# Products of two groups at once in the gates stage of a two-block layer: blind prediction and result

## The chip, the cores and the metric

The kernel runs on one core of a Trainium2 chip. The metric is the device time of one execution in microseconds; a time that is compared is the median of several runs. The core has five engines that take their instructions from queues of their own, each in the order in which the program issued them: TensorE (PE in the profile, with its weight loads as PEld), VectorE (DVE), ScalarE (ACT), GpSimd (POOL) and SyncE (SP), which here only starts DMAs.

## The reference

Two transformer blocks on 256 tokens of width 1024 in float32. The first has a SwiGLU layer, a hybrid of stick-breaking attention and a state-space mixer, cross attention and a second SwiGLU layer. The second has a mixer and then an expert layer with 16384 experts of rank one, which is the part that matters here:

```python
q = (xt @ wq).reshape(t, PEER_HEADS, 2, HALF_Q)
scores = jnp.einsum('thpd,hpnd->thpn', q, keys)
s_top, i_top = lax.top_k(scores, PEER_TOPK)          # 16 of 128 keys, twice
...                                                  # 16 of the 256 sums: c_score, c_idx
expert = i1 * N_KEYS + i2                            # 8 heads x 16 experts a token
gates = jax.nn.softmax(c_score, axis=-1)
u = jnp.take(u_tab, eb, axis=0)
a = jax.nn.gelu(jnp.einsum('td,thkd->thk', xb, u), approximate=False)
w = gb * a
y = jnp.einsum('thk,thkd->td', w, jnp.take(v_tab, eb, axis=0))
```

## The kernel before, in words

The kernel doesn't gather experts. It computes the Gelu of every token with all 16384 rows of the first table (the units `pu`, 128 tiles of 128 experts), multiplies by a dense matrix of gates, mostly zeros, and multiplies the result with the whole second table (the units `pv`). X holds 128 x 128 x 256 values: first index i1's tile, partition i2, then the token.

A tile of `pu` is one call of `f_tile` (L324): 24 matmuls (L332 to L334, three for each of 8 parts of the width, since a float32 weight is split in a rounded `hi` and a rest `lo`) into one of two PSUM banks `mm`. Then ScalarE applies the Gelu (L1488 into X for tokens whose gates are not there yet, L1490 in place for the others) and VectorE multiplies the latter into X (L1491). The split of a later tile's weights is made at a tile's end: `hi` on ScalarE (L169), `lo` on VectorE (L170).

The dense gates are made beside these tiles, four tokens (a group) at a time, 64 groups, by the generator `gates` (L1366). For each token of a group GpSimd compares a row of numbers with the first index (`m1`, L1375, one-hot), ScalarE scales it by the gate's upper part (`oh`, L1377), VectorE by its lower part (`ol`, L1380), and VectorE makes the one-hot of the second index (`m2`, L1378). All this is `hot`. TensorE multiplies `oh` and `ol` with `m2` (L1388, 8 matmuls of 128 columns a group, float16) into a PSUM bank `sd`, of which there are two. Then the group is spread over X: ScalarE copies the gates of tiles that have no Gelu yet (L1396), VectorE multiplies the others into X (L1398). The tiles `m1`, `m2`, `oh` and `ol` have two buffers each.

What sets the order is a planner. Each generator has a time due. `f_tile` calls `tick(1.3)` in the middle of a tile (behind 12 matmuls) and at its end, behind the Gelu and the product and ahead of the split; a tick takes 1.3 from the time due and, as long as it isn't above zero, steps the generator and adds what that yields. A step without a number adds 3.3 here, so a group comes every 3.3 us of the planner's time. One step before issues the products of group g, then `hot` of g + 1, then the spread of g.

Of the kernel before, what the change touches and what calls it, by code (L numbers as in the profile page):

```python
# [8 lines left out]
F16 = mybir.dt.float16  # L9
I32 = mybir.dt.int32  # L10
U32 = mybir.dt.uint32
AF = mybir.ActivationFunctionType
OP = mybir.AluOpType
# [103 lines left out]
class Builder:  # L117
# [363 lines left out]
    def spread(self, hn, t, dst, col):  # L481
        self.transposes(hn[t].ap, t, dst, col)
        hn[t].free()
# [882 lines left out]
    def gates(self, kT, X):  # L1366

        nc = self.nc

        def hot(g):  # L1370
            tile = lambda name: self.pw.tile([128, 4, 128], F16, name=name, bufs=2)
            m1, m2, oh, ol = (tile(n) for n in ("m1", "m2", "oh", "ol"))
            key = lambda w, i: kT[:, w, 4 * g + i:4 * g + i + 1]
            for i in range(4):
                nc.gpsimd.tensor_scalar(m1[:, i], self.iota, key(0, i), None, op0=OP.is_equal)  # L1375
            for i in range(4):
                nc.scalar.activation(oh[:, i], m1[:, i], AF.Copy, scale=key(2, i))  # L1377
                nc.vector.tensor_scalar(m2[:, i], self.iota, key(1, i), 1.0 / self.SCALE, op0=OP.is_equal, op1=OP.mult)  # L1378
            for i in range(4):
                nc.vector.tensor_scalar(ol[:, i], m1[:, i], key(3, i), None, op0=OP.mult)  # L1380
            return (oh, ol), m2
        o = hot(0)
        yield
        for g in range(64):
            ps = self.sd()
            for i in range(4):
                for p in range(2):
                    nc.tensor.matmul(ps[:, i * 128:i * 128 + 128], o[0][p][:, i], o[1][:, i], start=(p == 0),  # L1388
                                     stop=(p == 1))
            if g < 63:  # L1390
                o = hot(g + 1)
            E = self.u_done
            pv = ps.rearrange("p (t i) -> p t i", t=4)
            x = X[:, :, 4 * g:4 * g + 4].rearrange("p i t -> p t i")
            if E < 128:
                nc.scalar.activation(x[:, :, E:128], pv[:, :, E:128], AF.Copy)  # L1396
            if E:
                nc.vector.tensor_mul(x[:, :, 0:E], pv[:, :, 0:E], x[:, :, 0:E])  # L1398
            self.g_done = 4 * g + 4
            yield  # L1400

    def peer(self):
        nc, hT = self.nc, self.uT
# [407 lines left out]
```

## Time and profile before

| | |
|---|---|
| median of 3 runs | 1656.46 us (1656.13 to 1656.62) |
| the profiled execution | 1655.53 us, its span 1653.8 us |
| PE, PEld busy | 1632.5 us (99%), 1481.6 us (90%) |
| DVE busy | 1148.0 us (69%) |
| ACT busy | 977.9 us (59%) |
| POOL busy | 268.6 us (16%) |
| DMA | 288.77 MB, mean 175 GB/s |
| chain that ended last | PE 81%, DVE 11%, ACT 3%, issue 2%, DMA 2%, POOL 1% |

Busy shares are means over the whole span. The gates stage lies between about 1024 and 1292 us from the start; GpSimd is busy almost only there. Matmuls are pipelined and their ends are modelled, so on TensorE one reads the starts: the distance from a start to the next is what a matmul costs.

### The profile page before, as it was taken

The page shows a single profiled execution, that of the slowest core. Times are in us where ns is not written, and L with a number is a line of the kernel's source. Part 1 is how long each engine was busy: PE and PEld are TensorE (multiplying, and loading weights), DVE is VectorE, ACT ScalarE, POOL GpSimd, SP SyncE. Part 2 cuts the span into 40 slices and gives each one's busy share as a digit, 9 for nine tenths or more (in the row PEclk, how much of TensorE's full clock was granted, in tenths as well). Part 3 has the DMA queues.
Part 4 walks back from the last instruction along what each step waited for, and adds up shares of the span by engine and source line. Part 5 has one row for each costly group of instructions (what it writes and reads, how often), then busy time and mean ns, then how long its engine had stood idle before and what let it go on. Part 6 is the DMA issues. An engine that isn't in the chain of part 4 may idle for free.

```text
span 1653.8 us, 29236 instructions
## 1 busy us (share of the span) xinstructions
PE 1632.5 (99%) x11102; PEld 1481.6 (90%) x11102; DVE 1148.0 (69%) x2366; ACT 977.9 (59%) x1826; POOL 268.6 (16%) x311
## 2 busy tenths in 40 slices
PE   8999999999999999999999999999999999999998
PEld 6999899988898899979889999999999888888886
DVE  6554765877756645487657998899999755555554
ACT  6443676786555544467355565888877555444454
POOL 0000000000000000000100003988888000000000
PEclk9999999999999999999999999999999999999999
DMA  7565643364524656555244555444454555555553
GB/s 280 192 208 175 227 143 116 115 202 143 179 103 154 216 190 206 177 185 197 78 140 143 192 190 192 166 163 164 161 166 153 180 205 194 194 195 193 191 191 128
DMA packets 79325, 288.77 MB, mean 175 GB/s; under 512 B 8784, under 2 KB 8912, under 8 KB 79056
## 3 DMA queue, kind: packets, MB, share of 16 engines
q1 hardware_dynamic: 77904, 281.66, 49.8%
q10 hardware_dynamic: 1280, 5.24, 1.0%
q8 instruction: 87, 1.43, 0.3%
q14 instruction: 54, 0.44, 0.1%
HBM read 285.82 MB, written 1.05 MB: 173 GB/s over the span
## 4 chain that ended last, share of the span: by engine, by line
PE 81%; DVE 11%; ACT 3%; issue 2%; DMA 2%; POOL 1%; SPq 0%; POOLq 0%; DVEq 0%; ACTq 0%
PE mm L332 12%; PE mm L334 12%; PE mm L333 12%; PE acc L349 10%; PE acc L351 10%; PE acc L353 10%; DVE lo L170 4%; PE mm L303 2%; PE mm L300 2%; PE mm L299 2%; DMA raw<-ws 2%; PE sd L1388 1%; ACT hi L169 1%; DVE m L1378 1%; DVE X L1260 1%
## 5 line engine op out<-in xcount | busy, mean ns | idle before, releaser
L170 DVE TENSOR_TENSOR lo<-raw,hi 128x1024 fp32r<-128x1024 f32 x414 | 506.6, 1228 | 237.5 <-ACT hi L169 236.1
L332 PE MATMUL mm<-uT,hi 128*128 128x256 f32 x2104 | 597.1, 284 | 2.1 <-DVE X L1491 1.7
L334 PE MATMUL mm<-uT,lo 128*128 128x256 f32 x2104 | 587.1, 279 | 0.0
L333 PE MATMUL mm<-uT,hi 128*128 128x256 f32 x2104 | 586.9, 279 | 0.0
L169 ACT ACTIVATE hi<-raw 128x1024 fp32r<-128x1024 f32 x414 | 436.3, 1058 | 214.9 <-PE acc L353 171.1
L332 PEld LDWEIGHTS mm<-uT,hi 128*128 128x128 f32 x2104 | 397.1, 189 | 4.9 <-DVE X L1491 2.6
L333 PEld LDWEIGHTS mm<-uT,hi 128*128 128x128 f32 x2104 | 397.1, 189 | 0.8
L334 PEld LDWEIGHTS mm<-uT,lo 128*128 128x128 f32 x2104 | 397.0, 189 | 0.0
L1375 POOL TENSOR_SCALAR m<-iota,kT 128x128 f16<-128x128 f16 x256 | 233.2, 927 | 197.8 <-DVE kT L1358 149.9
L438 POOL TENSOR_TENSOR hr<-hv,mhalf 128x1 f32<-128x1 f32 x26 | 14.4, 552 | 816.3 <-DVE hv L437 816.3
L349 PE MATMUL acc<-hi,wf 128*128 128x512 f32 x384 | 118.9, 390 | 0.0
L351 PE MATMUL acc<-lo,wf 128*128 128x512 f32 x384 | 118.7, 389 | 0.0
L353 PE MATMUL acc<-hi,wf 128*128 128x512 f32 x384 | 118.5, 389 | 0.0
L170 DVE TENSOR_TENSOR lo<-fa,hi 128x1024 fp32r<-128x1024 f32 x69 | 84.1, 1233 | 34.0 <-ACT hi L169 33.7
L531 ACT ACTIVATE fa<-mm 128x256 f32<-128x256 f32 x36 | 13.8, 383 | 122.9 <-PE mm L334 122.9
L351 PEld LDWEIGHTS acc<-lo,wf 128*128 128x128 f32 x384 | 72.1, 188 | 15.2
L353 PEld LDWEIGHTS acc<-hi,wf 128*128 128x128 f32 x384 | 72.1, 188 | 15.1
L349 PEld LDWEIGHTS acc<-hi,wf 128*128 128x128 f32 x384 | 72.1, 188 | 14.9
L1488 ACT ACTIVATE X<-mm 128x256 f32<-128x256 f32 (+40 forms) x126 | 39.6, 314 | 76.0 <-PE mm L334 75.0
L1377 ACT ACTIVATE oh<-m,kT 128x128 f16<-128x128 f16 x256 | 81.1, 390 | 0.0
L169 ACT ACTIVATE hi<-fa 128x1024 fp32r<-128x1024 f32 x69 | 70.7, 1051 | 5.6 <-PE mm L303 3.1
L1398 DVE TENSOR_TENSOR X<-sd,X 128x184 f32<-128x184 f32 (+31 forms) x64 | 60.9, 951 | 1.2 <-ACT X L1396 1.1
(364 smaller groups left out, 2550.9 us busy)
## 6 DMA issues: line engine op xcount, KB each, us to landing
raw<-ws SPq DMA_DIRECT2D x442, 512.0 KB, 3.3
fa<-ws SPq DMA_DIRECT2D x91, 512.0 KB, 4.4
fa<-rows ACTq DMA_DIRECT2D x5, 512.0 KB, 4.7
fa<-mem ACTq DMA_DIRECT2D x1, 1024.0 KB, 7.7
X<-keysT ACTq DMA_DIRECT2D x1, 1024.0 KB, 5.0
out<-X SPq DMA_DIRECT2D x4, 256.0 KB, 2.0
h<-x SPq DMA_DIRECT2D x2, 256.0 KB, 2.8
h<-x SPq DMA_DIRECT2D x1, 512.0 KB, 7.3
```

Of the source, the lines that this page charges most:

```text
L169: nc.scalar.activation(hi, raw, AF.Copy)
L170: nc.vector.tensor_sub(lo, raw, hi.bitcast(F32))
L332: nc.tensor.matmul(ps, wh, ah[:, k, :], start=(k == 0), stop=False)
L333: nc.tensor.matmul(ps, wh, al[:, k, :], start=False, stop=False)
L334: nc.tensor.matmul(ps, wl, ah[:, k, :], start=False, stop=(k == 7))
L349: nc.tensor.matmul(o[h], ah[:, k, ts], hi[:, hs[h]], start=first, stop=False)
L351: nc.tensor.matmul(o[h], ah[:, k, ts], lo[:, hs[h]], start=False, stop=False)
L353: nc.tensor.matmul(o[h], al[:, k, ts], hi[:, hs[h]], start=False, stop=last)
L1375: nc.gpsimd.tensor_scalar(m1[:, i], self.iota, key(0, i), None, op0=OP.is_equal)
L1377: nc.scalar.activation(oh[:, i], m1[:, i], AF.Copy, scale=key(2, i))
L1398: nc.vector.tensor_mul(x[:, :, 0:E], pv[:, :, 0:E], x[:, :, 0:E])
L1488: nc.scalar.activation(X[:, i, g:256], ps[:, g:256], AF.Gelu)
```

## The change

The products of two groups are issued in one step, into both `sd` banks, and the first one-hots (`ones`) of the next two groups right behind them on GpSimd. The two spreads and then the two `hot`s follow as steps of their own, 0.9, 1.3, 0.7 and 1.6 us of the planner's time apart, and 2.1 behind the last of them the next products. Two groups take 6.6 us of it, as before.

```diff
-        def hot(g):
-            tile = lambda name: self.pw.tile([128, 4, 128], F16, name=name, bufs=2)
-            m1, m2, oh, ol = (tile(n) for n in ("m1", "m2", "oh", "ol"))
-            key = lambda w, i: kT[:, w, 4 * g + i:4 * g + i + 1]
+        tile = lambda name: self.pw.tile([128, 4, 128], F16, name=name, bufs=2)
+        key = lambda g, w, i: kT[:, w, 4 * g + i:4 * g + i + 1]
+
+        def ones(g):
+            m1 = tile("m1")
             for i in range(4):
-                nc.gpsimd.tensor_scalar(m1[:, i], self.iota, key(0, i), None, op0=OP.is_equal)
+                nc.gpsimd.tensor_scalar(m1[:, i], self.iota, key(g, 0, i), None, op0=OP.is_equal)
+            return m1
+
+        def hot(g, m1):
+            m2, oh, ol = (tile(n) for n in ("m2", "oh", "ol"))
...
-        o = hot(0)
-        yield
-        for g in range(64):
+
+        def products(o):
             ps = self.sd()
             for i in range(4):
                 for p in range(2):
                     nc.tensor.matmul(ps[:, i * 128:i * 128 + 128], o[0][p][:, i], o[1][:, i], start=(p == 0),
-                                     stop=(p == 1))
-            if g < 63:
-                o = hot(g + 1)
+                                    stop=(p == 1))
+            return ps
+
+        def spread(g, ps):
             E = self.u_done
...
             self.g_done = 4 * g + 4
-            yield
+        o = [hot(g, ones(g)) for g in range(2)]
+        yield
+        for g in range(0, 64, 2):
+            pss = [products(p) for p in o]
+            more = g + 2 < 64
+            m1 = [ones(g + 2 + i) for i in range(2)] if more else []
+            o = []
+            for i, us in enumerate((0.9, 1.3)):
+                yield us
+                spread(g + i, pss[i])
+            for i, us in enumerate((0.7, 1.6)):
+                yield us
+                if more:
+                    o.append(hot(g + 2 + i, m1[i]))
+            yield 2.1
```

## Rows read from the trace of the kernel before

**Rows 1.** Stretches: us; busy (count) of PE, PEld, DVE, ACT, POOL; PE's clock; DMA
```profile
1030.00:1100.00 70.00, 70.00 (x658) 69.29 (x657) 62.83 (x193) 61.85 (x151) 63.58 (x71) 1.00 0.48 163
1100.00:1200.00 100.00, 100.00 (x939) 99.01 (x937) 97.81 (x286) 82.87 (x214) 86.55 (x98) 1.00 0.49 164
1200.00:1290.00 90.00, 88.56 (x811) 85.92 (x811) 90.00 (x241) 68.12 (x186) 71.12 (x80) 1.00 0.46 155
```

**Rows 2.** Waits in the gates stage, 1024 to 1292 us: total, times, longest
```profile
POOL m L1375 <- DVE ol L1380: 44.0, 46, 14.6
...
PE mm L332 <- DVE X L1491: 1.7, 4, 0.5
...
DVE X L1398 <- ACT X L1396: 1.1, 4, 0.4
...
PEld L1388 <- DVE ol L1380: 0.3, 1, 0.3
```

**Rows 3.** TensorE in order of time: start, duration, line; groups 0, 19, 20, 62
```profile
1028.52 0.23 PE L1388 MATMUL sd<-m,oh 128*128 128x128 f16 x1
...
1106.20 0.23 PE L1388 MATMUL sd<-m,oh 128*128 128x128 f16 x1
...
1106.60 0.22 PE L1388 MATMUL sd<-m,ol 128*128 128x128 f16 x1
1106.63 0.37 PE L332 MATMUL mm<-uT,hi 128*128 128x256 f32 x1
1106.84 0.28 PE L333 MATMUL mm<-uT,hi 128*128 128x256 f32 x1
1106.95 0.28 PE L334 MATMUL mm<-uT,lo 128*128 128x256 f32 x1
...
1109.55 0.23 PE L1388 MATMUL sd<-m,oh 128*128 128x128 f16 x1
...
1285.91 0.23 PE L1388 MATMUL sd<-m,oh 128*128 128x128 f16 x1
```

**Rows 4.** Groups by line, 1030 to 1290 us: count, busy us, mean ns
```profile
L1375 POOL TENSOR_SCALAR m<-iota,kT 128x128 f16<-128x128 f16 x247 | 221.9, 915 | 33.3 <-DVE ol L1380 29.4 <-ACT X L1396 1.4 <-ACT oh L1377 1.0
```

**Rows 5.** ScalarE in order of time, group 19
```profile
1106.88 1.27 ACT L1377 ACTIVATE oh<-m,kT 128x128 f16<-128x128 f16 x4
1108.05 0.58 ACT L1396 ACTIVATE X<-sd 128x232 f32<-128x232 f32 x1
1108.42 1.07 ACT L169 ACTIVATE hi<-raw 128x1024 fp32r<-128x1024 f32 x1
```

**Rows 6.** VectorE in order of time, group 19 and (from 1222.60) group 47
```profile
1104.81 0.79 DVE L1398 TENSOR_TENSOR X<-sd,X 128x272 f32<-128x272 f32 x1
1105.52 0.22 DVE L1491 TENSOR_TENSOR X<-X,mm 128x76 f32<-128x76 f32 x1
...
1107.00 0.23 DVE L1491 TENSOR_TENSOR X<-X,mm 128x76 f32<-128x76 f32 x1
1107.15 0.85 DVE L1378 TENSOR_SCALAR m<-iota,kT 128x128 f16<-128x128 f16 x4
1107.85 0.84 DVE L1380 TENSOR_SCALAR ol<-m,kT 128x128 f16<-128x128 f16 x4
1108.66 0.82 DVE L1398 TENSOR_TENSOR X<-sd,X 128x280 f32<-128x280 f32 x1
1109.52 1.35 DVE L170 TENSOR_TENSOR lo<-raw,hi 128x1024 fp32r<-128x1024 f32 x1
...
1222.60 1.21 DVE L170 TENSOR_TENSOR lo<-raw,hi 128x1024 fp32r<-128x1024 f32 x1
1223.73 0.85 DVE L1378 TENSOR_SCALAR m<-iota,kT 128x128 f16<-128x128 f16 x4
1224.50 0.73 DVE L1380 TENSOR_SCALAR ol<-m,kT 128x128 f16<-128x128 f16 x4
```

**Rows 7.** TensorE in order of time, the last product of group 48
```profile
1225.29 0.23 PE L1388 MATMUL sd<-m,ol 128*128 128x128 f16 x1
```

More of the change, by code (lines that the diff above doesn't have):

```diff
@@ L1368, in gates @@
         nc = self.nc
-        def hot(g):
-            tile = lambda name: self.pw.tile([128, 4, 128], F16, name=name, bufs=2)
-            m1, m2, oh, ol = (tile(n) for n in ("m1", "m2", "oh", "ol"))
-            key = lambda w, i: kT[:, w, 4 * g + i:4 * g + i + 1]
+        tile = lambda name: self.pw.tile([128, 4, 128], F16, name=name, bufs=2)
+        key = lambda g, w, i: kT[:, w, 4 * g + i:4 * g + i + 1]
+        def ones(g):
+            m1 = tile("m1")
             for i in range(4):
-                nc.gpsimd.tensor_scalar(m1[:, i], self.iota, key(0, i), None, op0=OP.is_equal)
+                nc.gpsimd.tensor_scalar(m1[:, i], self.iota, key(g, 0, i), None, op0=OP.is_equal)
+            return m1
+        def hot(g, m1):
+            m2, oh, ol = (tile(n) for n in ("m2", "oh", "ol"))
             for i in range(4):
-                nc.scalar.activation(oh[:, i], m1[:, i], AF.Copy, scale=key(2, i))
-                nc.vector.tensor_scalar(m2[:, i], self.iota, key(1, i), 1.0 / self.SCALE, op0=OP.is_equal, op1=OP.mult)
+                nc.scalar.activation(oh[:, i], m1[:, i], AF.Copy, scale=key(g, 2, i))
+                nc.vector.tensor_scalar(m2[:, i], self.iota, key(g, 1, i), 1.0 / self.SCALE, op0=OP.is_equal, op1=OP.mult)
             for i in range(4):
-                nc.vector.tensor_scalar(ol[:, i], m1[:, i], key(3, i), None, op0=OP.mult)
+                nc.vector.tensor_scalar(ol[:, i], m1[:, i], key(g, 3, i), None, op0=OP.mult)
             return (oh, ol), m2
-        o = hot(0)
-        yield
-        for g in range(64):
+        def products(o):
             ps = self.sd()
```

## The prediction

> **What bounds the kernel now.** The table by stretches comes first [rows 1]: TensorE (PE) is busy all the time up to 1200 and 88.56 of 90 us behind, at a granted clock of 1.00, so its instruction stream sets the end. In the gates stage this is close to failing: VectorE (DVE) is busy 62.83 of 70 us from 1030, 97.81 of 100 from 1100, and 90.00 of 90 from 1200. There two engines are full, and TensorE gets along only because VectorE's results come just in time. The waits of the gates stage [rows 2] say how seldom they don't: TensorE waited 1.7 us for the product L1491, and its weight load 0.3 us for `ol`, in the whole stage. The 44.0 us that GpSimd waits for `ol` cost nothing, since nobody in the list waits for GpSimd.
>
> Next TensorE in order of time [rows 3]. Products start at 1028.52 (group 0) and 1285.91 (group 62): 257.4 us for 62 groups, 8.30 us a pair. One group costs TensorE the 0.43 us from its first matmul to the next tile's first, and 0.09 more because the second matmul after the change of type comes 0.21 later instead of 0.12: 0.52, call it 0.51 with the rounding. From 1106.20 to 1109.55 lie one tile and one group, so half a tile (12 matmuls) is (3.35 - 0.51) / 2 = 1.42 us. 3.3 us of the planner's time a group at 1.3 a half tile are 2.54 half tiles, 157 in 62 groups: 157 x 1.42 + 62 x 0.51 = 254.6, so under 3 us of the 257.4 are waits. That is all that better order can win here, besides cheaper products.
>
> **What the products gain.** A second group right behind the first costs eight steps more, 0.45 (seven are 0.40, 1106.20 to 1106.60 [rows 3]), instead of 0.51: 0.96 a pair, 0.06 saved, 1.9 us in 31 pairs. Instructions are the same in number and shape on every engine; no DMA is added or moved. GpSimd's eight one-hots a pair take 8 x 0.915 = 7.3 us [rows 4], which fits a pair of 8.1 and more, and start as soon as the tiles come free: hidden by the rest of the pair, with about 0.8 us to spare; were that cover gone, ScalarE's `oh` would wait for them. Both PSUM banks are free for the next pair once S1 is done, two ticks or more ahead of P: no wait there.
>
> **What the order costs.** Each engine takes its queue in order, and I follow the queue from a tile's end to the products. I write P for the products, S0 and S1 for the two spreads, H0 and H1 for the two `hot`s. They are due at 0, 0.9, 2.2, 2.9, 4.5 and again P at 6.6, and each is issued at the first tick (half tile, 1.3) at or behind its due time. A pair is 6.6 / 1.3 = 5.08 ticks; P's lateness within its tick moves by 0.1 a pair, so 13 pairs go through all phases. Ticks of S0, S1, H0, H1, next P:
> A, 4 pairs of 13: 0, 1, 2, 3, 5.
> B, 3: 1, 2, 2, 3, 5.
> C, 3: 1, 2, 2, 4, 5.
> D, 2: 1, 2, 3, 4, 5.
> E, 1: 1, 2, 3, 4, 6.
> In 8 of 13 the last `hot` is issued two half tiles ahead of the products that need it, in 5 only one. Before it was two or three, at the head of the queue, with the spread behind it.
>
> Durations come from group 19, whose products begin at a tile's end, 1106.20. ScalarE (ACT) has its two Gelus done and is free 0.68 later (1106.88), VectorE is through L1491 0.95 later (1107.15) [rows 5, 6]. `oh` takes ScalarE 1.17 (1106.88 to 1108.05), the spread's copy 0.58 to its end and 0.37 to the next start, the split's `hi` 1.07. VectorE: a `hot` 1.54 from its first `m2` to the end of its last `ol`, 1.51 to the next instruction; the spread's product 0.71 (1104.81 to 1105.52), L1491 0.15, the split's `lo` 1.13 (1222.60 to 1223.73). The spread's product waits for the spread's copy [rows 2], `lo` for `hi` (1108.42 + 1.07, then 1109.52). And products follow `ol` closely: `ol` ended at 1225.23, the last product began at 1225.29 [rows 6, 7], so P is done 0.10 behind the last `ol`.
>
> Case A with P at a tile's end: the tile behind P ends at 0.96 + 2 x 1.42, and from there: `oh` 0.68 to 1.85, `hi` to 2.92, `lo` (queued behind H0) 2.95 to 4.08, H1 to 5.62, P done 5.72. From P's end to the next P's end: 2.84 + 5.72 = 8.56. TensorE alone needs 5 x 1.42 + 0.96 = 8.06: it waits 0.5.
> Case A with P inside a tile: the tile ends 1.42 behind P; then copy to 1.26, S1's product to 2.00, `hi` to 2.12, `lo` to 3.28, H0 to 4.79, L1491 to 4.94, H1 to 6.48, P 6.58: 8.00, no wait, 8.06.
> Case B, tile's end: S1 is now queued behind the Gelus: copy 1.26, product 2.00, H0 3.51, `lo` 4.64 (`hi` 3.29), H1 6.18, P 6.28: 9.12. Inside: S0's product 2.00, `lo` 3.28, S1's product 3.99, H0 5.50, L1491 5.65, H1 7.19, P 7.29: 8.71.
> Case C: L1491 of one more tile (tile's end), or `lo` too (inside), slips in ahead of H1: 9.27 and 9.84. D: H0 is behind the `lo` instead of ahead of it. Tile's end: `lo` 3.28, H0 4.79, L1491 4.94, H1 6.48, P 6.58: 9.42. Inside: S1's product 3.99, L1491 4.14, H0 5.65, `hi` 5.75, `lo` 6.91, H1 8.45, P 8.55: 9.97. E: 9.48, which is TensorE's own 6 x 1.42 + 0.96, and 9.97.
> Both positions alternate, so the means are 8.31, 8.92, 9.56, 9.70, 9.73, and over the 13: (4 x 8.31 + 3 x 8.92 + 3 x 9.56 + 2 x 9.70 + 9.73) / 13 = 9.06. 31 pairs: 280.9 against 257.4, so **+23.5 us**; the 1.9 gained by the products is in it, since 0.96 stands in each pair.
>
> What is late next, by this: ScalarE and VectorE idle at the tile's end in front of the Gelu, because H0 and H1 were put behind it, and TensorE waits in the second half of the joint products. Who is queued behind: the next tiles, so nothing catches up. The ends: at the start H1 of the first pair adds about 0.6 (1.54 of VectorE's time against 0.96 of products and what is left); at the end a wait for L1491 (0.5 at the longest [rows 2]) may go. I take these two as nil, within 0.6 either way. Unknown are the hand-overs: five in a chain, 0.03 to 0.1 each in these rows, so 0.3 a pair, 9 us in all. The late spreads have longer products and shorter copies, since the tiles move from the one to the other; within the same 9.
>
> The profiled execution took 1655.53 us for a span of 1653.8; the median is 1656.46, 0.06% above, so the sum is put on the median: 1656.5 + 23.5 = **1680**, its own range 1671 to 1689.
>
> A rule that would make it worse. The granted clock is 1.00 in all rows, waits of up to 0.5 us included [rows 1, 2]. If waits of 0.5 to 1.9 us, 31 times, brought the clock down to 1.2 GHz for the half tile behind each, that half tile would take 2.84 instead of 1.42: 31 x 1.42 = 44 us on top, 1724. The Trainium skill (TensorE: Matmul & The Clock Gate, Part 1: The HAM clock gate) says that the throttled clock is the default and that only activity keeps it away. By that rule the longer waits are a danger; the trace so far, with TensorE still over 85% busy in my layout, speaks against it.
>
> **Rivals.** *Faster: the order has room.* If H0 and H1 are always done when TensorE comes (VectorE's queue being emptier at that point than I lay out, as `hot` was in time for nearly all groups before [rows 2]), only gains are left: 1.9 from the products and the 3 us of waits, as the work on VectorE is now spread: 1651.5. Against it: a `hot` is 1.54 and H1 begins behind a tile's Gelu, a `hot` and mostly a `lo`; it decides in this rival's favour if the chain from the tile's end is done within the 5.22 (3 x 1.42 + 0.96) that TensorE takes, where I have 5.72 (case A, tile's end).
> *No change: VectorE was full anyway.* Where it is busy 90 of 90 us, a wait of TensorE costs nothing that VectorE would not have cost. This holds only for the third behind 1200; if it held from 1100 on, the loss would be confined to the first third, a few us against the 5 gained: within 3 us of 1656.5. Against it: 97.81% of 8.30 is 8.12 us of VectorE's work a pair, which leaves it 0.9 idle in 9.06.
> *Much slower: waits feed each other.* A late L1491 holds the mm bank for the tile after next. That wait exists now, 0.5 at the longest [rows 2]; one of 0.5 in each pair on top adds 15.5: 1695.
>
> **How the numbers follow.** Forecast 0.63; faster 0.16; no change 0.08; much slower 0.10; the clock 0.03. A change under 0.2% (3.3 us) can't be told from none. Slower is 0.63 + 0.10 + 0.03 = 0.76, which is beyond 1659.8. The range leaves out the faster case and the clock: 1654 to 1696; the likeliest case alone is 1671 to 1689.
>
> **What would show it.** Products at a pair's second group should start late: a gap inside L1388, at matmul 9 of 16, with `ol` of H1 ending 0.1 ahead of the end of P, and the waits of PEld and PE for `ol` (L1380) growing from 0.3 to tens of us. The distance from products to products should be 8.1 to 10 with the phase, longest where S1 and H0 fall on one tick and H1 on the last before P. VectorE's busy share from 1200 should fall below 95%. GpSimd's waits may change without effect. The prediction is wrong in its mechanism if the pairs keep 8.1 to 8.3, and in size if waits of case A (half a us) stand in all pairs (+8) or if L332 waits for L1491 in most.

## The result, and the profile after

The changed kernel took **1681.08 us** (median of 4 runs, 1677.92 to 1682.61) against 1656.3 for the kernel before on the same chip: ratio 1.0149, 95% interval 1.0137 to 1.0161. The forecast was 1680, with a range of 1654 to 1696. The profiled execution's span is 1679.2 us, 25.4 more than before; the 82 tiles of `pu` that run beside the gates took 293.2 us from the first matmul to the last (1029.72 to 1322.92) instead of 268.6, so 24.6 of the 25.4 arose there.

The changed kernel's lines: `ones` L1376, `oh` L1382, `m2` L1383, `ol` L1385, products L1392, the spread's copy L1401 and product L1403, Gelu L1507 and L1509, L1510 for what was L1491.

Its busy time by stretches (columns as in [rows 1]); the last two are cut out around the places where the granted clock fell:

```profile
1030.00:1100.00 70.00, 66.90 (x609) 63.44 (x608) 59.20 (x186) 56.60 (x142) 53.93 (x65) 1.00 0.45 155
1100.00:1200.00 100.00, 94.71 (x851) 90.29 (x851) 86.67 (x253) 73.74 (x194) 74.57 (x89) 0.98 0.43 146
1200.00:1300.00 100.00, 92.25 (x818) 87.33 (x818) 90.61 (x237) 66.79 (x187) 73.29 (x86) 0.98 0.42 143
...
1118.00:1126.00 8.00, 7.83 (x55) 7.68 (x56) 4.40 (x10) 3.58 (x10) 4.67 (x7) 0.79 0.38 133
...
1217.00:1225.00 8.00, 6.62 (x45) 6.40 (x45) 5.11 (x14) 2.27 (x8) 6.18 (x8) 0.79 0.38 131
```

VectorE, full before from 1200 [rows 1], is busy 90.61 of 100 us: it does the same work in more time. TensorE's matmul counts fell from 939 to 851 in the same 100 us. So neither engine is at its limit, and something makes them wait for each other. The waits of the changed kernel, 1024 to 1320 us (columns as in [rows 2]):

```profile
DVE X L1510 <- ACT mm L1509: 27.8, 25, 3.4
PEld L1392 <- DVE ol L1385: 25.5, 31, 2.2
...
PE sd L1392 <- DVE ol L1385: 11.6, 24, 0.7
...
PE sd L1392 <- DVE m L1383: 5.9, 10, 1.2
```

The two sides of one thing: TensorE's products wait for `ol` and `m2` (before: 0.3 us [rows 2]), and VectorE waits, in front of a tile's product, for that tile's Gelu, 27.8 us (3.3 before), which comes late because TensorE came late. No wait of L332 for the product L1510 is in the list any more. Of the kernel before (1024 to 1292 us), beside [rows 2]:

```profile
DVE X L1491 <- ACT mm L1490: 3.3, 6, 0.7
PEld mm L332 <- DVE X L1491: 2.6, 5, 0.7
```

One wait for `m2` and `ol`, in the products of groups 20 and 21 in the changed kernel's TensorE queue, in order of time (start, duration; in brackets the idle time before it and what ended that):

```profile
1115.72 0.23 PE L1392 MATMUL sd<-m,oh 128*128 128x128 f16 x1
...
1116.12 0.22 PE L1392 MATMUL sd<-m,ol 128*128 128x128 f16 x1
1117.48 0.22 PE L1392 MATMUL sd<-m,oh 128*128 128x128 f16 x1 [1.14 <-DVE m L1383]
1118.17 0.23 PE L1392 MATMUL sd<-m,ol 128*128 128x128 f16 x1 [0.48 <-DVE ol L1385]
...
1118.66 0.23 PE L1392 MATMUL sd<-m,ol 128*128 128x128 f16 x1
```

The first eight run through. The ninth, the first of group 21, begins 1.36 us after the eighth instead of 0.06, and the tenth 0.69 after it. What VectorE did meanwhile:

```profile
1111.08 0.23 DVE L1510 TENSOR_TENSOR X<-X,mm 128x72 f32<-128x72 f32 x1 [1.28 <-ACT mm L1509]
1111.60 0.82 DVE L1403 TENSOR_TENSOR X<-sd,X 128x276 f32<-128x276 f32 x1 [0.29 <-ACT X L1401]
1112.47 1.22 DVE L170 TENSOR_TENSOR lo<-raw,hi 128x1024 fp32r<-128x1024 f32 x1
1113.61 0.80 DVE L1403 TENSOR_TENSOR X<-sd,X 128x276 f32<-128x276 f32 x1
1114.32 0.22 DVE L1510 TENSOR_TENSOR X<-X,mm 128x80 f32<-128x80 f32 x1
1114.47 0.73 DVE L1383 TENSOR_SCALAR m<-iota,kT 128x128 f16<-128x128 f16 x4
1115.12 0.72 DVE L1385 TENSOR_SCALAR ol<-m,kT 128x128 f16<-128x128 f16 x4
1115.92 1.23 DVE L170 TENSOR_TENSOR lo<-raw,hi 128x1024 fp32r<-128x1024 f32 x1
1117.07 0.85 DVE L1383 TENSOR_SCALAR m<-iota,kT 128x128 f16<-128x128 f16 x4
1117.84 0.77 DVE L1385 TENSOR_SCALAR ol<-m,kT 128x128 f16<-128x128 f16 x4
```

and ScalarE:

```profile
1110.83 0.21 ACT L1509 ACTIVATE mm<-mm 128x72 f32<-128x72 f32 x1
1110.95 0.61 ACT L1401 ACTIVATE X<-sd 128x236 f32<-128x236 f32 x1
1111.34 1.10 ACT L169 ACTIVATE hi<-raw 128x1024 fp32r<-128x1024 f32 x1
...
1113.68 1.27 ACT L1382 ACTIVATE oh<-m,kT 128x128 f16<-128x128 f16 x4
1114.85 1.04 ACT L169 ACTIVATE hi<-raw 128x1024 fp32r<-128x1024 f32 x1
```

This is the prediction's chain of case D inside a tile, link by link. VectorE has idled 1.28 us when the tile's Gelu is done (1111.04). S0's product waits for its copy (1111.56, then 1111.60), `lo` for `hi` (1112.44, then 1112.47), S1's product behind it, L1510, H0, the second `lo` for its `hi` (1115.89, then 1115.92), and only then H1, whose last `ol` ends at 1118.6; the last product starts 0.05 later. No single link is slow. The second `hot` simply stands last in a row of eight pieces that could not begin before the tile's end.

### The profile page after: what moved, and what is told of

Same layout as the page of the kernel before. It is cut to its first block, busy times and chain, and to the rows that moved or that the text cites. A ratio compares the mean times of both kernels' runs of the same rounds, so it can differ in the third digit from the quotient of the medians.

```text
span 1679.2 us, 29225 instructions
## 1 busy us (share of the span) xinstructions
PE 1641.2 (98%) x11102; PEld 1480.6 (88%) x11102; DVE 1147.6 (68%) x2366; ACT 973.3 (58%) x1825; POOL 255.3 (15%) x311
## 3 DMA queue, kind: packets, MB, share of 16 engines
HBM read 285.82 MB, written 1.05 MB: 171 GB/s over the span
## 4 chain that ended last, share of the span: by engine, by line
PE 83%; DVE 8%; ACT 4%; issue 3%; DMA 1%; POOL 0%; SPq 0%; POOLq 0%; DVEq 0%; ACTq 0%
PE mm L332 13%; PE mm L334 13%; PE mm L333 13%; PE acc L349 10%; PE acc L351 10%; PE acc L353 10%; DVE lo L170 2%; PE mm L303 2%; PE mm L300 2%; PE mm L299 2%; DVE m L1383 2%; PE sd L1392 2%; DVE ol L1385 1%; ACT hi L169 1%; DVE X L1403 1%
## 5 line engine op out<-in xcount | busy, mean ns | idle before, releaser
L332 PE MATMUL mm<-uT,hi 128*128 128x256 f32 x2104 | 594.6, 283 | 0.6 <-ACT X L1507 0.6
L332 PEld LDWEIGHTS mm<-uT,hi 128*128 128x128 f32 x2104 | 398.8, 190 | 2.2 <-ACT X L1507 0.8
L1376 POOL TENSOR_SCALAR m<-iota,kT 128x128 f16<-128x128 f16 x256 | 220.0, 877 | 234.9 <-DVE kT L1358 149.8
L1507 ACT ACTIVATE X<-mm 128x256 f32<-128x256 f32 (+39 forms) x125 | 39.0, 312 | 106.6 <-PE mm L334 106.3
L351 PEld LDWEIGHTS acc<-lo,wf 128*128 128x128 f32 x384 | 72.1, 188 | 15.2
L1382 ACT ACTIVATE oh<-m,kT 128x128 f16<-128x128 f16 x256 | 80.9, 393 | 0.0
L1403 DVE TENSOR_TENSOR X<-sd,X 128x184 f32<-128x184 f32 (+31 forms) x64 | 61.2, 956 | 4.0 <-ACT X L1401 3.6
```

Source lines behind the costliest of these rows:

```text
L332: nc.tensor.matmul(ps, wh, ah[:, k, :], start=(k == 0), stop=False)
L351: nc.tensor.matmul(o[h], ah[:, k, ts], lo[:, hs[h]], start=False, stop=False)
L1376: nc.gpsimd.tensor_scalar(m1[:, i], self.iota, key(g, 0, i), None, op0=OP.is_equal)
L1507: nc.scalar.activation(X[:, i, g:256], ps[:, g:256], AF.Gelu)
```

## The experiments

Theory D, the distance: TensorE waits because the last piece that the next products need is issued only 2.1 us of the planner's time ahead of them. Rivals: J, that two groups' products in a row with both banks taken at once cost the time; O, that the spread stands ahead of the tiles; V, that VectorE is full and sets the pace anyway. In each diff the minus lines are of the changed kernel unless said otherwise.

**Joint products, the rest in the order of before (`pair_only`).**

```diff
-            more = g + 2 < 64
-            m1 = [ones(g + 2 + i) for i in range(2)] if more else []
             o = []
-            for i, us in enumerate((0.9, 1.3)):
-                yield us
+            for i in range(2):
+                if g + 2 < 64:
+                    o.append(hot(g + 2 + i, ones(g + 2 + i)))
                 spread(g + i, pss[i])
-            for i, us in enumerate((0.7, 1.6)):
...
-            yield 2.1
+                yield 3.3
```

> Joint products of two groups, but the rest in the order of before: hot of g+2 and spread of g in the same step as the products, hot of g+3 and spread of g+1 3.3 later. Theory D (the distance: TensorE waits because the last hot is issued only 2.1 of the planner's time ahead of the products that need it): the last hot is 3.3 ahead again, as before the change, so no waits inside the products; 0.06 saved in each of 31 pairs: 1652 to 1657, pairs 8.1 to 8.4. Rival J (two groups' products in a row, with both banks taken at once, cost the time themselves): about 1675 to 1682. Rival V (VectorE is full, its work sets the pace whatever the order): nothing to do with the order, so the loss of 25 us can't come from it and J or something else must hold.

Measured: 1655.68 us, ratio to before 1.0001 (0.9992 to 1.0010). All 25 us are gone with the joint products kept, so J falls as the cause of the loss, and V too. One thing came otherwise than expected: there are waits inside the products, 6.2 us in 16 of the 31 pairs, all in front of the ninth. They are not for a `hot` but for the PSUM bank: each time the ninth product starts 0.05 us behind the end of the second spread's product, while the last `ol` had ended 0.66 us or more ahead of it. So joint products are not free; both banks must be empty at once. Two lines of this kernel's waits, 1030 to 1300 us (`issue` means that the profile shows nothing that the weight load waited for):

```profile
PEld L1392 <- issue: 5.2, 13, 0.9
...
PE sd L1392 <- DVE X L1403: 1.7, 5, 0.6
```

**The spread ahead of `hot`, one group at a time (`spread_first`).** The minus and plus lines are of the kernel before.

```diff
-            if g < 63:
-                o = hot(g + 1)
             E = self.u_done
...
                 nc.vector.tensor_mul(x[:, :, 0:E], pv[:, :, 0:E], x[:, :, 0:E])
+            if g < 63:
+                o = hot(g + 1)
```

> The kernel before, one group at a time, with only the order inside a step turned: the spread of g ahead of hot of g+1. Theory D: hot ends one copy and one product later (about 0.7 to 1.0 us), against 0.2 to 2 us of room before; the distance stays 3.3: 1656 to 1661. A rival O (that the spread stands ahead of the tiles is the cause, whatever the distance): a good part of the 25 us, 1668 or more.

Measured: 1656.40 us, 1.0005 (0.9996 to 1.0015). The order inside a step is worth nothing that can be measured: O falls.

**The same steps closer to the products (`close_steps`).**

```diff
-            for i, us in enumerate((0.9, 1.3)):
+            for i, us in enumerate((0.0, 0.65)):
...
-            for i, us in enumerate((0.7, 1.6)):
+            for i, us in enumerate((0.65, 1.3)):
...
-            yield 2.1
+            yield 4.0
```

> The changed kernel with only its due times moved: spreads at 0 and 0.65 behind the products, hots at 1.3 and 2.6 instead of 2.9 and 4.5, the next products at 6.6 as ever. Same order of everything, same joint products. Theory D: the last hot is three half tiles ahead of the products, no waits inside them: 1653 to 1660, with perhaps some waits of the next tile for L1491, since VectorE gets its work in one heap. Rivals J and O: no change from the changed kernel, 1677 to 1683.

Measured: 1655.63 us, 1.0000 (0.9991 to 1.0009). Only numbers were changed, five due times; the pieces of the gates stand in the same order among themselves, and each engine has as many instructions as in the changed kernel (ScalarE one fewer; the widths of copies and products shift as the tiles move past them). This is the plainest proof of D: the loss goes with the distance.

**The second group's products half a tile later (`split_products`).**

```diff
-            pss = [products(p) for p in o]
+            pss = [products(o[0])]
+            second = o[1]
...
+            yield 0.9
+            spread(g, pss[0])
+            yield 0.4
+            pss.append(products(second))
+            yield 0.9
+            spread(g + 1, pss[1])
```

> The changed kernel with only the second group's products issued one half tile (1.3) behind the first's; spreads and hots due as in the changed kernel. Theory D: the wait is for the last hot, and stands at the second group; it gets 1.42 us more, so it stays only in cases C and D with the products inside a tile (0.4 to 0.5 each): 1657 to 1663. Rival J: it is gone as well, but all of it, and the waits for ol inside the products too. Rival V: VectorE's pace holds, at least 1670. Rival O: 1677 or more.

Measured: 1656.19 us, 1.0005 (0.9996 to 1.0014), just below what was expected. With the spreads and `hot`s at their changed times, half a tile of other work between the two products takes nearly all of the wait. Waits of this kernel from 1030 to 1300:

```profile
PEld L1392 <- DVE ol L1385: 1.7, 5, 0.6
...
PE sd L1392 <- DVE ol L1385: 1.0, 4, 0.4
```

**The second `hot` 1.0 later (`far_step`).**

```diff
-            for i, us in enumerate((0.7, 1.6)):
+            for i, us in enumerate((0.7, 2.6)):
...
-            yield 2.1
+            yield 1.1
```

> The changed kernel with only the second hot due 1.0 later, 1.1 ahead of the next products instead of 2.1. Theory D, by the same layout of the queues: in A and B it slips one half tile and one more L1491 or lo stands ahead of it (A 8.31 to 8.9 a pair, B 8.92 to 9.56), in D and E too (to 10.3), C stays at 9.56: mean 9.53 instead of 9.06, +15 us: 1692 to 1702. Longer waits may bring the clock down more often than twice, 1.7 us each. Rival J or O: no change, 1677 to 1683.

Measured: 1696.63 us, 1.0254 (1.0238 to 1.0270) of before, where the changed kernel is 1.0149: 1.05% or 17 us more (15.5 between the medians), where the layout of the queues gave 15. The granted clock fell twice in this stage, as in the changed kernel. Its waits, 1024 to 1340:

```profile
PEld L1392 <- DVE ol L1385: 37.7, 37, 2.2
...
PE sd L1392 <- DVE ol L1385: 15.1, 31, 0.7
PE sd L1392 <- DVE m L1383: 12.7, 16, 1.4
```

**`hot`s and spreads in each other's places (`hots_first`).**

```diff
             for i, us in enumerate((0.9, 1.3)):
                 yield us
-                spread(g + i, pss[i])
+                if more:
+                    o.append(hot(g + 2 + i, m1[i]))
             for i, us in enumerate((0.7, 1.6)):
                 yield us
-                if more:
-                    o.append(hot(g + 2 + i, m1[i]))
+                spread(g + i, pss[i])
```

> The changed kernel with the two hots in the places of the two spreads and the other way round, due times kept. What is 2.1 ahead of the next products is now the second spread, which must be done with its PSUM bank before the next products may write it. Theory D in its wide form (whatever the next products need must not be issued that late, hot or spread): the chain ends with a copy and a product of 0.71 instead of a hot of 1.54, but the products can't overlap with it; by the layout A 8.06, B 8.9, C 9.5, D 9.7, E 9.9, mean 8.96: 1670 to 1680, with waits of TensorE for the spread's product. Theory D in its narrow form (only the hot counts) and rival O: 1653 to 1660.

Measured: 1686.10 us, 1.0182 (1.0167 to 1.0198), above the expected range. The direction decides for the wide form: whatever the next products need must not be issued that late. Here it is the PSUM bank (waits, 1024 to 1330): in 28 of 31 pairs the ninth product starts 0.05 us behind the end of the second spread's product. And in the profiled execution the clock fell five times (stretches):

```profile
PE sd L1392 <- DVE X L1403: 25.1, 33, 1.7
```

```profile
1100.00:1130.00 30.00, 26.36 (x217) 25.83 (x215) 20.87 (x68) 18.63 (x50) 19.07 (x25) 0.89 0.39 129
...
1222.00:1250.00 28.00, 22.84 (x189) 22.32 (x186) 21.30 (x58) 14.59 (x40) 16.46 (x22) 0.88 0.39 132
...
1310.00:1320.00 10.00, 8.14 (x64) 7.91 (x63) 8.16 (x24) 5.11 (x15) 3.37 (x6) 0.83 0.50 161
```

30 x 0.11 + 28 x 0.12 + 10 x 0.17 = 8.4 us of full clock are missing there. But this execution is the slowest of the four, 1692.16 us; less 8.4 it would be about 1684 (arithmetic, no run shows it), and the other three, at a mean clock of 0.997 to 0.998, took 1683.34 to 1686.41. So the falls alone don't explain the miss: the waits are longer than the layout had them. One part of that is seen: the layout had let the first group's products through, and they waited too, 9.7 us in all between the last matmul of a tile and the first product.

**Where the cheaper products went (`before_lighter`, `close_lighter`).** `pair_only` and `close_steps` should have gained 1.9 us and gained nothing. Counted from the first product to the 53rd of the 82 tiles, a stretch with 42 groups in each kernel, the kernel before took 168.6 us (1028.52 to 1197.15) and `close_steps` 167.1 (1029.28 to 1196.38): 1.5 gained in 21 pairs, where 0.06 a pair gives 1.3. So the gain is there. `pair_only` took 168.8 (1028.75 to 1197.54): its waits for the bank, 2.5 us in this stretch, ate it up. The last 30 tiles took 100.4 us before and 101.2 in `close_steps`, with waits that stand almost only behind 1197 (1197 to 1300):

```profile
PEld mm L332 <- DVE X L1510: 4.6, 8, 1.4
PE mm L332 <- DVE X L1510: 3.0, 5, 1.2
```

That is where VectorE is full [rows 1]. Theory F: there its work sets the pace. So one of four `ol` products was given to ScalarE from group 32 on, in the kernel before and in `close_steps` (the lines are of the former):

```diff
-            for i in range(4):
+            s = 3 if g >= 32 else 4
+            for i in range(s, 4):
+                nc.scalar.activation(ol[:, i], m1[:, i], AF.Copy, scale=key(3, i))
+            for i in range(s):
                 nc.vector.tensor_scalar(ol[:, i], m1[:, i], key(3, i), None, op0=OP.mult)
```

> The kernel before with one of the four ol products of each group from 32 on made by ScalarE instead of VectorE (0.2 us less for VectorE a group). If VectorE's work sets the pace behind 1200 and not the order (theory F), the waits of the last 22 groups (about 3.5 us together) go: 1652 to 1654. If ScalarE's extra 0.3 a group delays the Gelus as much: no change.

> The close steps (joint products, due times 0, 0.65, 1.3, 2.6) with the same lightening from group 32 on. Theory F: joint products save 0.06 a pair, which close_steps gained up to 1196 and gave back behind it; with VectorE relieved it keeps it: 1649 to 1653, faster than both kernels. Otherwise 1655.

Measured: 1652.47 us, 0.9983 (0.9974 to 0.9992), and 1652.04 us, 0.9983 (0.9974 to 0.9992). Both beat the kernel before and the changed one; between them nothing can be told. The difference to the kernel before is 0.17%: small, but the interval does not reach 1. F holds for the kernel before: the last 30 tiles took 97.2 us in `before_lighter`, 3.2 less than before, and the first 52 the same 168.2. TensorE from 1200 to 1290 in `before_lighter`, against 88.56 before [rows 1]; VectorE's busy share hardly shows the relief, 89.81 against 90.00:

```profile
1200.00:1290.00 90.00, 89.64 (x837) 88.11 (x836) 89.81 (x224) 76.08 (x212) 71.08 (x80) 1.00 0.48 161
```

`close_lighter` gains ahead of them as `close_steps` does: 167.2 us from the first product to the 53rd tile (1029.52 to 1196.75), against 168.6 in `before_lighter` (1028.93 to 1197.57). But it needs 98.5 for the last 30, 1.3 more, with waits that the other has got rid of (1190 to 1300; first `close_lighter`, then `before_lighter`):

```profile
PEld mm L332 <- DVE X L1513: 2.6, 6, 0.7
...
PEld mm L332 <- DVE X L1494: 0.7, 2, 0.5
```

So the joint products' gain is real and eaten up in the last 30 tiles, and that a relieved VectorE would let it last is not borne out.

## Why the prediction was right

**The chain.** Distances from the start of one pair's last product to that of the next, in the changed kernel, by case and place of the pair that is left, against the layout (31 distances, in us; the two with a star hold a fall of the clock):

```
case, place      layout  measured
A, tile's end     8.56   8.62 8.52 8.72 8.68 9.06 9.24
A, inside         8.06   8.01 8.00 8.04 8.04 8.11
B, tile's end     9.12   9.10 9.03 9.19
B, inside         8.71   8.50 8.65 8.86 8.91 9.53
C, tile's end     9.27   9.02 8.90 9.13 10.65*
C, inside         9.84   9.72 10.29
D, tile's end     9.42   10.88* 9.38
D, inside         9.97   9.94 10.39
E, inside         9.97   9.96 10.56
mean of the 31    8.97   9.15
```

Case by case the layout holds. Each line is in order of time, and the last entries are mostly the high ones, by 0.4 to 0.8: that fits the longer product of the late spreads, which I had left within the bounds (not tested by itself). C at a tile's end came out 0.1 to 0.4 shorter. Together the 29 without a star are 2.7 us longer than the layout.

That the total agrees so well is in part luck. The forecast's mean of 9.06 took the cases as 4 : 3 : 3 : 2 : 1 and both places as equally frequent; in the 31 distances the short case A came 11 times and E twice, both times inside. With these counts the layout gives 8.97, 2.8 us less in all than was forecast. The longer links (2.7) and the two falls of the clock (2.8 in the starred distances) made up for that and more: 283.6 us measured, 280.9 forecast.

**The row of links.** For the pair shown above the layout, counted from its tile's end at 1110.2, puts the end of the first `lo` at 1113.5, of S1's product at 1114.2, of H0 at 1115.9, of the second `lo` at 1117.1 and of H1 at 1118.7; the next instruction or the end came at 1113.61, 1114.32, 1115.9, 1117.07 and 1118.6.

**The signs named.** The waits for `ol` in tens of us and VectorE under 95% are there, and the last product starts 0.06 to 0.09 us behind the last `ol` in nearly all pairs. Of 31 pairs 28 waited by 0.1 us or more inside the products. The gap named, at matmul 9 of 16, is there in 15 pairs, 8.6 us in all; the larger wait stands one product later, at the tenth, the first that needs an `ol` of H1: 26 pairs, 15.9 us.

**The clock.** I had given 0.03 to a fall behind every wait, at 44 us. It fell twice, in the stretches at 0.79: 2 x 8 x 0.21 = 3.4 us of full clock lost, from 1.00 to a mix with its lower level, 1.2 GHz. The first came right behind the wait shown above, the second at the end of one in which one gap was 1.47 us. Another of the same kind, at 1236.7, with a gap of 1.41, had none. The rule of the Trainium skill (TensorE: Matmul & The Clock Gate, Part 1: The HAM clock gate), that the lower clock is the default and activity keeps it away, agrees with these two; in the other 26 pairs that waited the clock stayed at 1.00.

**What was off.** The 1.9 us that the joint products gain were taken as a plain term. The experiments show that without the waits they would not have lasted to the end of the stage. The rival that VectorE is full anyway was wrong for the change, whose last 30 tiles lost 9.4 us (109.8 against 100.4) beside 15.2 in the first 52; it is right for the kernel before and for `close_steps` in the last 30 tiles. The rival of waits for the mm bank did not come about in the changed kernel; it did in `close_steps`. The longest such wait before was 0.7 and not 0.5 us: I had left out the weight loads' row, shown above. I said the longest distances would be those of C; D and E inside a tile are as long, and my own layout had them longer (9.97 against 9.84).

## What to carry to other kernels

In queues that run in order, the room for a result is the distance from where it is issued to where it is needed, less everything that stands between its own inputs and it; spreading work evenly over a period uses up that room, even though no engine gets more to do. Put what the next round needs at the head of the period, its inputs and the buffers that it must find empty. And where two engines are both nearly full, a saving on the first shows only once the second is relieved: one `ol` in four, moved from VectorE to ScalarE in half of the groups, was worth 2.8 us, where no reordering here won anything measurable over the kernel before.

## What was not expected of the hardware

The granted clock fell although TensorE was busy 94.71 and 92.25 of 100 us in the stretches around it and no single gap between its matmuls was above 1.5 us. In the profiled execution of `hots_first`, with the bank waits, it fell five times in the stage, though its gaps inside the products are of similar size (1.88 at the longest); in `far_step`, with gaps up to 1.66, twice.

The same wait does not always bring a fall. At about 797 us, well ahead of the gates stage, where all the kernels are alike, TensorE waits 1.21 us for VectorE (L1127) in each of the ten profiled executions. In those of `spread_first` and `hots_first` the clock fell right behind it, in the other eight it did not. The stretch in the kernel before, then in `spread_first`:

```profile
790.00:800.00 10.00, 8.79 (x82) 8.47 (x81) 7.84 (x19) 3.41 (x6) 1.01 (x1) 1.00 0.32 107
...
790.00:800.00 10.00, 8.79 (x71) 8.47 (x69) 7.63 (x18) 3.41 (x6) 1.01 (x1) 0.84 0.33 107
```

So the length of the wait alone does not tell; what does stays open here.
